# Feed-forward layers and a query projection: seven products over eight input tiles instead of four or six, with two of the weight sums made by adding transfers

## The chip, the core and the metric

The kernel runs on one core of one Trainium2 chip. The metric is device time in microseconds of the whole program, the median of several runs. On the core, TensorE (PE) multiplies, VectorE (DVE) and ScalarE (ACT) work element by element, GpSimd (POOL) does a few small operations, and the queues of SyncE (SP) and POOL issue transfers between memory and the chip.

## What is computed

The input is 256 rows of 2048 numbers in float32. Two layers follow each other. Cut to what matters here:

```python
D_MODEL = 2048; SEQ = 256; D_FF = 8192; N_HEADS = 16
def sq_relu_mlp(h, g, w1, w2):
    a = relu(rms_norm(h, g) @ w1)          # 2048 -> 8192
    return (a * a) @ w2                    # 8192 -> 2048
# layer 1: q, k, v, gate from one projection, causal attention with a forget bias
h = h + attention_1(h) @ a_w_out
h = h + sq_relu_mlp(h, mlp_norm_g[0], mlp_w1[0], mlp_w2[0])
# keys and values shared by what follows
k_sh, v_sh = split(rms_norm(h, kv_norm_g) @ kv_w)
# layer 2: own queries, chunked attention with a relative bias
q = rms_norm(rms_norm(h, b_norm_g) @ b_w_q)
h = h + attention_2(q, k_sh, v_sh) @ b_w_out
h = h + sq_relu_mlp(h, mlp_norm_g[1], mlp_w1[1], mlp_w2[1])
```

## The kernel before, in words

**Tiles.** The 256 rows are two blocks b of 128 (`NB`). The 2048 inputs of a product are 16 tiles of 128 (`KT`), its outputs panels of 512 columns. A weight comes in units of 128 x 1024 numbers (512 KB): two input tiles by one panel.

**Three passes.** Each unit is split into a coarse part `hi` (ScalarE, L210) and the rest `lo` (VectorE, L211) by `issue`, and activations are kept split in the same way. `passes` (L443 to L448) multiplies high by high, low by high and high by low; so a plain unit takes 2 blocks x 2 input tiles x 3 = 12 matmuls of 128 x 512. `fetch` (L220) keeps up to three split units ahead of TensorE (three `hi` and three `lo` buffers in pool `wsp`), and `EARLY` = 3 raw units loading beyond (`load`, L193, pool `wraw`, four buffers).

**Pairs in seven products.** In the feed-forward layers two neighbouring panels (1024 columns) make a `Pair` (L120). For the first n of the 16 input tiles the two row blocks by two panels are computed in seven products in place of eight, in Winograd's arrangement: blocks 11, 12, 21, 22 of the weight (input half by panel) and sums of them, T1 = 12 - 11, T3 = 22 - 12, T2 = T3 + 11, T4 = 21 - T2, each meet an activation block or a sum of activation blocks (`sums`, L262, kept in tiles `S` and `Sh`). The other 16 - n tiles are plain units, named a and b by panel. In the first weight n is 4 and a block is 1024 wide; in the second weight ("wide") n is 6 and a block is 1536 wide, split in one step of 1024 and one of 512 (`hih`, `loh`). `form_products` (L467) issues the matmuls of a block: 6 for 1024 numbers, 3 for 512.

`bring` (L777 to L779) loads whole blocks on the SP queue, `make` (L790) forms the sums T1 to T4 on VectorE, each pair at times given in `units` to each `Pair` (L153 to L165) and kept by `prepare`. Between the products the accumulators are folded: ScalarE copies them (L879, L882), VectorE adds (L861, L865).

**Chunks.** A feed-forward layer runs in four chunks (`NCH`) of 2048 hidden columns: two pairs of the first weight, then two pairs of the second, which use what the first two gave. `turn_hidden` (L825) transposes a finished panel in 32 x 32 pieces (L314), sends it out to memory and back (`turn`, L324 and L330), and `take` (L800) applies ReLU and square and splits (L803 to L814). The panels of the second weight are added to the rows h (L561). `plan_mlp` (L145) lists all units of a layer in order; the units b5 to b7 of a pair are put among the first products of the next.

**Other stages.** `panels` (L479) and `stage` (L496) run the other projections with plain units only, the query projection of layer 2 (`w_qb`, four panels) among them. Small work is handed out step by step through `fill` (`add_fill`, `run_fill`), one list of steps after each unit. `next_x` (L342) prepares the next stage's activations at the steps given in `LONG` and `SHORT`. `keep_order` (L36) holds DVE, ACT, PE and SP to the order in which the program is written, so an instruction that waits holds all that is behind it on its engine.

Of the kernel before, what the change touches and what calls it, by code (L numbers as in the profile page):

```python
# [15 lines left out]
P = 128  # L16
# [13 lines left out]
EARLY = 3  # L30
UA = UN // 512
REL = 384
WIDE = UN + 512
# [14 lines left out]
def trunk(ctx: ExitStack, tc: tile.TileContext, xT, xr, gs, hg, bf, wgate, w_in, w_oa, w1a, w2fa, w2sa,  # L48
          w_kv, w_qb, w_ob, w1b, w2fb, w2sb, rel, out):
# [9 lines left out]
    wraw = pool("wraw", 4)  # L59
    qkv = pool("qkv", 2)  # L60
    wk = pool("wk", 6)
# [46 lines left out]
    class Form:  # L108

        def __init__(self, pair, i, half):  # L110
            self.pair, self.name, self.half = pair, ("11", "T3", "T2", "T1", "21", "T4", "22")[i], half

    class Tail:

        fast = None

        def __init__(self, src, first):
            self.src = [[src[first + u] for u in range(KT // UA)]]

    class Pair:  # L120

        fast = True

        def __init__(self, big, src, order, third, units):
            self.big, self.src, self.third, self.units, self.order = big, src, third, units, order
            self.ps, self.t, self.wide, self.own = None, {}, order == "wide", 3 if order == "wide" else 2

        def items(self, names):
            return [(self, "abfh".index(i[0]), int(i[1])) for i in names.split()]

        def plan(self, rest):
            made = [self.items(f"f{i} h{i}" if self.wide else f"f{i}") for i in range(7)]
            own = {"early": "a2 F a3 F b2 F b3 a4 b4 a5 a6 a7", "": "a2 F a3 F a4 F a5 a6 a7 b2 b3 b4",
                   "wide": "a3 F b3 F a4 F b4 a5 a6 a7"}[self.order].split()
            plan = made[0] + rest[:1] + made[1] + rest[1:2] + made[2] + rest[2:] + made[3]
            n = 4
            for i in own:
                if i == "F":
                    plan += made[n]
                    n += 1  # L140
                else:
                    plan += self.items(i)
            return plan, self.items("b5 b6 b7")

    def plan_mlp(w1, w2f, w2s, tail):  # L145
        n, pairs = w1.shape[0] // NCH, []
        names = ("11", "12", "21", "22")
        for c in range(NCH):
            for q in range(2):
                at = c * n + 16 * q  # L150
                src = [[w1[at + 8 * j + u] for u in range(8)] for j in range(2)]
                order = "" if pairs else "early"
                when = (25, 20, 9, 15, 10, 8) if not pairs else (9, 7, 8, 6, 3, 2) if q and not c else (9, 7, 8, 6, 5, 1) if q else (7, 5, 6, 4, 3, 2)  # L153
                pairs.append(Pair({k: src[int(k[1]) - 1][int(k[0]) - 1] for k in names}, src, order, len(pairs) % 2 == 0, when))
            for q in range(2):
                at = 2 * c + q
                src = [[None] * 3 + [w2s[10 * at + 5 * j + u] for u in range(5)] for j in range(2)]
                when = (7, 5, 6, 4, 3) if q else (9, 7, 8, 6, 5) if c else (9, 7, 8, 6, 3)
                pairs.append(Pair({k: w2f[4 * at + i] for i, k in enumerate(names)}, src, "wide", len(pairs) % 2 == 0, when))
        plan, rest = [], [(tail, 0, u) for u in range(KT // UA - 3, KT // UA)]  # L160
        for p in pairs:
            mine, rest = p.plan(rest)
            plan += mine
        plan += rest
        units.extend(Form(p, i, q == 3) if q > 1 else p.src[q][i] for p, q, i in plan)  # L165
        return plan
# [3 lines left out]
    n_out = w_oa.shape[0] - 3  # L170
    queue(w_oa, n_out)
    tail_a = Tail(w_oa, n_out - 5)
    plan_a = plan_mlp(w1a, w2fa, w2sa, tail_a)
    queue(w_qb, w_qb.shape[0])
# [3 lines left out]
    tail_b = Tail(w_ob, n_out - 5)  # L178
    plan_b = plan_mlp(w1b, w2fb, w2sb, tail_b)
# [4 lines left out]
    def load(parts=1):  # L184
        src = units.popleft()
        if isinstance(src, Form):
            raws.append((src, ()))
            return
# [5 lines left out]
        raws.append((raw, cuts))  # L194

    def issue(parts=1):
        form = None
        if not raws:
            load(parts)
        raw, cuts = raws.popleft()  # L200
        if not cuts:
            form, half = raw, raw.half
            raw, cuts = form.pair.t[form.name], [slice(0, 512 if half else UN)]
            if half:
                raw = raw[:, UN:]
        n = cuts[-1].stop
        hi = wsp.tile([P, n], F32R, name="hi" if n == UN else "hih", bufs=3 if n == UN else 1)
        lo = wsp.tile([P, n], F32R, name="lo" if n == UN else "loh", bufs=3 if n == UN else 1)
        for c in cuts:
            S.activation(hi[:, c], raw[:, c], AF.Copy)  # L210
            V.tensor_tensor(lo[:, c], raw[:, c], hi[:, c].bitcast(F32), op=ALU.subtract)  # L211
        ready.append((hi, lo, n < UN))
        if form and form.name == "T3" and half == form.pair.wide:
            make(form.pair, "T2")

    def half_next():
        u = raws[0][0] if raws else units[0]
        return isinstance(u, Form) and u.half

    def fetch(ahead=AHEAD, early=EARLY):  # L220
        while (units or raws) and sum(1 for r in ready if not r[2]) <= ahead and not (half_next() and any(r[2] for r in ready)):
            issue()
        while units and sum(1 for r in raws if r[1]) < early:
            load()
        return ready.popleft()[:2]
# [14 lines left out]
    def acc_pair(which=None):  # L240
        if which is None:
            which, turns[0] = turns[0], 1 - turns[0]
        if which == 2:
            return [ps_s.tile([P, 512], F32, name="s") for _ in range(2)]
        return [ps_acc.tile([P, 512], F32, name="acc", tag=f"acc{which}{b}", bufs=1) for b in range(NB)]
# [16 lines left out]
    def sums(a, fs, n=2):  # L262

        w = [wk.tile([P, 512], F32, name="sum", tag="wk") for _ in range(n)]

        def part(i):
            at = i * n * P
            v = w[at // 512][:, at % 512 : at % 512 + n * P].rearrange("p (g t) -> p g t", g=n)
            return v.rearrange("p g (i c) -> p g i c", i=4) if len(a[0][0].shape) == 4 else v

        V.tensor_tensor(part(0), a[1][0], a[1][1], op=ALU.add)
        V.tensor_tensor(part(1), part(0), a[0][0], op=ALU.subtract)
        V.tensor_tensor(part(2), a[0][0], a[1][0], op=ALU.subtract)
        V.tensor_tensor(part(3), a[0][1], part(1), op=ALU.subtract)
        hi, lo = ([fs[k][:, i * 512 : (i + 1) * 512] for i in range(n)] for k in range(2))
        for i in range(n):
            S.activation(hi[i], w[i], AF.Copy)
        yield
        for i in range(n):
            V.tensor_tensor(lo[i], w[i], hi[i].bitcast(F32), op=ALU.subtract)  # L280
        yield

    def room(tag, name, dtype=F32):
# [729 lines left out]
```

## Time and profile before

| what | value |
|---|---|
| median of 3 runs | 2126.61 us (2125.93 to 2134.7) |
| profiled execution, from the first to the last instruction (its span) | 2124.3 us |
| PE, PEld, DVE busy | 2101.3, 1729.3, 1654.6 us |
| ACT, POOL busy | 1211.3, 49.1 us |
| granted TensorE clock, mean | 0.999 |
| moved by transfers | 491.63 MB, 231 GB/s on average |
| read from memory, written | 450.01 MB, 39.87 MB |

The first feed-forward layer runs from about 372 to 1062 us, the queries follow up to about 1115 us, keys, values and attention up to about 1390 us, and the second output projection and feed-forward layer fill the rest. A group's row gives line, engine, operation, output and inputs with their shapes, the count, then the busy time in us and the mean of one in ns, and last the idle time before them with what ended it. A timeline's row gives start, length, engine, line, operation and, in brackets, the idle time just before. PE's matmuls are pipelined: they overlap, and the time between their starts is what one costs.

### The profile page before, as it was taken

To read this page: it belongs to the slowest core of one execution; us is meant where nothing else is said; L and a number is where in the kernel's file an instruction comes from. 1 tells how busy PE (TensorE), PEld (TensorE's weight loads), DVE (VectorE), ACT (ScalarE), POOL (GpSimd) and SP (SyncE) were. 2 spreads that over 40 slices of the span, in tenths; PEclk is the share of its full clock that TensorE was granted. 3 is DMA by queue.
4 is the path that set the end of the run, shared out by engine and by line. 5 is a ranking of instruction groups with operands and counts; after the bars stand their busy time and mean duration, and the time that the engine had idled before them with its cause. 6 is when DMAs were issued, how large, how long until landed. Compare 5 with 4: busy or idle time off the path is not lost.

```text
span 2124.3 us, 26113 instructions
## 1 busy us (share of the span) xinstructions
PE 2101.3 (99%) x9278; PEld 1729.3 (81%) x9278; DVE 1654.6 (78%) x1931; ACT 1211.3 (57%) x1519; POOL 49.1 (2%) x48
## 2 busy tenths in 40 slices
PE   9999999999999999999999999999999999999999
PEld 7888888877888887888788888888788878878887
DVE  5767776888788878878877677678887887888786
ACT  6544445665566566556575454456654655665664
POOL 1001000000000000000001010000000000000000
PEclk9999999999999999999999999999999999999999
DMA  8787788776676576477577777787766766765763
GB/s 281 244 249 243 224 264 255 238 246 210 220 256 206 200 265 228 170 239 269 181 240 261 234 228 235 239 276 237 247 211 217 241 203 222 248 212 195 261 234 129
DMA packets 179283, 491.63 MB, mean 231 GB/s; under 512 B 36416, under 2 KB 73424, under 8 KB 179152
## 3 DMA queue, kind: packets, MB, share of 16 engines
q1 hardware_dynamic: 179152, 489.96, 69.8%
q8 instruction: 73, 1.20, 0.2%
q14 instruction: 58, 0.48, 0.1%
HBM read 450.01 MB, written 39.87 MB: 231 GB/s over the span
## 4 chain that ended last, share of the span: by engine, by line
PE 84%; DVE 7%; DMA 4%; ACT 2%; issue 2%; SPq 1%; ACTq 0%; DVEq 0%
PE acc L446 23%; PE acc L448 23%; PE acc L444 23%; PE s L444 4%; PE s L446 4%; PE s L448 4%; DVE lo L211 3%; ACT hi L210 2%; DVE w L790 1%; DVE loh L211 1%; DMA q<-turn 1%; DMA turn<-z 1%; DMA raw<-in_w_in 1%; DVE wT L790 1%; PE s L583 1%
## 5 line engine op out<-in xcount | busy, mean ns | idle before, releaser
L211 DVE TENSOR_TENSOR lo<-raw,hi 128x1024 fp32r<-128x1024 f32 (+1 forms) x610 | 738.2, 1215 | 260.1 <-ACT hi L210 253.0
L210 ACT ACTIVATE hi<-raw 128x1024 fp32r<-128x1024 f32 (+1 forms) x610 | 640.8, 1053 | 367.3 <-PE acc L446 266.8
L444 PE MATMUL acc<-hi,act 128*128 128x512 f32 x2208 | 608.4, 394 | 2.0 <-ACT hi L210 1.1
L446 PE MATMUL acc<-hi,act 128*128 128x512 f32 x2208 | 599.7, 390 | 6.4 <-DVE act L814 6.4
L448 PE MATMUL acc<-lo,act 128*128 128x512 f32 x2208 | 598.4, 390 | 0.0
L446 PEld LDWEIGHTS acc<-hi,act 128*128 128x128 f32 x2208 | 413.4, 188 | 98.2 <-DVE act L814 10.7
L448 PEld LDWEIGHTS acc<-lo,act 128*128 128x128 f32 x2208 | 413.3, 188 | 89.0 <-DVE lo L211 3.2
L444 PEld LDWEIGHTS acc<-hi,act 128*128 128x128 f32 x2208 | 412.9, 188 | 87.9 <-ACT hi L210 2.1
L210 ACT ACTIVATE hi<-w 128x1024 fp32r<-128x1024 f32 x160 | 169.1, 1057 | 226.4 <-DVE w L790 105.2
L211 DVE TENSOR_TENSOR lo<-w,hi 128x1024 fp32r<-128x1024 f32 x160 | 194.8, 1218 | 83.9 <-ACT hi L210 83.8
L444 PE MATMUL s<-hi,act 128*128 128x512 f32 x416 | 112.6, 389 | 0.0
L446 PE MATMUL s<-hi,act 128*128 128x512 f32 x416 | 112.5, 389 | 0.0
L448 PE MATMUL s<-lo,act 128*128 128x512 f32 x416 | 112.5, 389 | 0.0
L210 ACT ACTIVATE hi<-wT 128x1024 fp32r<-128x1024 f32 x64 | 67.7, 1057 | 54.9 <-DVE wT L790 27.9
L448 PEld LDWEIGHTS s<-lo,act 128*128 128x128 f32 x416 | 78.1, 188 | 16.2
L446 PEld LDWEIGHTS s<-hi,act 128*128 128x128 f32 x416 | 78.1, 188 | 16.2
L444 PEld LDWEIGHTS s<-hi,act 128*128 128x128 f32 x416 | 78.0, 188 | 16.2
L211 DVE TENSOR_TENSOR lo<-wT,hi 128x1024 fp32r<-128x1024 f32 x64 | 78.2, 1222 | 9.4 <-ACT hi L210 7.5
L210 ACT ACTIVATE hih<-w 128x512 fp32r<-128x512 f32 x80 | 49.8, 622 | 24.2 <-PE acc L446 16.0
L617 ACT ACTIVATE act<-po 128x256 fp32r<-128x256 f32 x32 | 12.3, 384 | 86.0 <-PE po L615 86.0
L211 DVE TENSOR_TENSOR loh<-w,hih 128x512 fp32r<-128x512 f32 x80 | 54.8, 685 | 7.3 <-ACT hih L210 7.3
L525 POOL TENSOR_TENSOR rn<-vv,mhalf 128x4 f32<-128x4 f32 x32 | 43.3, 1366 | 385.0 <-DVE vv L524 384.9
(190 smaller groups left out, 1717.0 us busy)
## 6 DMA issues: line engine op xcount, KB each, us to landing
raw<-in_w1a SPq DMA_DIRECT2D x96, 512.0 KB, 4.4
raw<-in_w1b SPq DMA_DIRECT2D x96, 512.0 KB, 4.5
raw<-in_w_in SPq DMA_DIRECT2D x94, 512.0 KB, 4.6
raw<-in_w2sa SPq DMA_DIRECT2D x80, 512.0 KB, 4.3
raw<-in_w2sb SPq DMA_DIRECT2D x80, 512.0 KB, 4.2
raw<-in_w_kv SPq DMA_DIRECT2D x64, 512.0 KB, 4.6
turn<-z SPq DMA_DIRECT2D x60, 512.0 KB, 4.2
w<-in_w2fa SPq DMA_DIRECT2D x32, 768.0 KB, 7.6
```

What stands on the lines that cost most here:

```text
L210: S.activation(hi[:, c], raw[:, c], AF.Copy)
L211: V.tensor_tensor(lo[:, c], raw[:, c], hi[:, c].bitcast(F32), op=ALU.subtract)
L444: TE.matmul(ps, xh, cut(hi, j), start=first, stop=False, **kw)
L446: TE.matmul(ps, xl, cut(hi, j), start=False, stop=False, **kw)
L448: TE.matmul(ps, xh, cut(lo, j), start=False, stop=last, **kw)
L525: G.tensor_tensor(rn, vv, mhalf, op=ALU.pow)
L583: TE.matmul(s[:, P : 3 * P], q[:, a, P:T], k[:, a], start=True, stop=True)
L617: S.activation(o[i][:, 0], po[:, :T], AF.Copy)
L790: V.tensor_tensor(d, a, b, op=op)
```

## The change

1. All pairs take n = 8: four tiles against four, blocks of 128 x 2048 ("11" to "22" in `f1a`, `f2a` and so on), each used in two halves s of 1024. A block half is one split step and 6 matmuls. The tile for `loh` and the 1536 wide blocks go. The activation sums are formed for both halves (`fs[0]`, `fs[1]`).
2. The query projection of layer 2 becomes two pairs as well, at the end of the first layer's plan.
3. The signs are arranged so that all sums of weights are additions: T3 = 12 + 22, T2 = T3 + 11, T1 = 11 + 12, T4 = T2 + 21. T3 and T1 are made by a transfer that adds block 22 (or 12) from memory into the tile of 12 (or 11), issued on the POOL queue. T2 and T4 stay on VectorE (L290, L260 of the new program). Blocks 21 and 22 as units of their own come through the raw buffers, so that 12 and 22 are read twice.
4. The order of the units is written out in `ORDER` for each kind of pair: f0 to f6 are the seven blocks (two halves each), a and b plain units, r the units left over from the pair before. What is brought, added and made after which unit, and how many units later, stands in `BEHIND`, and for the first pair of a layer in `OPENING`.
5. Accumulators alternate between `acc` and the banks of the pools `s` and `po`; two matmuls open two of them in the first pair of a layer. The last four units (before: three) of an output projection move into the plan behind it. Raw buffers: 6 for 4, `EARLY` 5 for 3, work buffers 5 for 6. The descriptor memory of POOL's queue is set to 8192.

In the program's order there are 8974 matmuls for 9138, 136 adding transfers on POOL, and 1269 transfers on SP for 1237; VectorE has 970 splits of 1024 for 830, none of 512 for 112, and 136 sums of weights of 1024 for 64 of 1024 and 64 of 1536.

```diff
-EARLY = 3
+EARLY = 5
+HIDDEN = ((1, 4, 7, 7, 8, 8, 10, 12), (1, 3, 7, 8, 8, 8, 11, 11), (1, 2, 5, 6, 6, 9), (0, 1, 4, 7, 7, 8))
+LONG = ((0, 0, 1, 3, 6, 7, 8, 8), (0, 0, 0, 1, 5, 5, 6, 6), (0, 0, 0, 0, 5, 6), (0, 0, 0, 2, 6, 6))
+SHORT = ((3, 0, 1, 3, 5, 5, 7, 8), (6, 1, 2, 5, 10, 10, 14, 14), (3, 0, 3, 4, 8, 10), (0, 0, 0, 2, 5, 5))
+ORDER = {
+    "first": "f0 r r f1 f2 r r f4 a4 f3 f5 b4 f6 a5 a6 r a7 b5",
+    "w10": "f0 r r f1 r f2 r f4 a4 a6 f3 a5 f5 f6 a7 b4 b5",
+    "w11": "f0 f1 r r f2 f4 a4 f3 a5 f5 f6 a6 a7 b4",
+    "w20": "r f0 r f1 f2 r f4 f3 f5 f6 a5 b4 a4 b5",
+    "w21": "f0 f1 f2 r f4 r f3 a5 r a4 b4 f6 r f5 a6",
...
+    "q0": "f0 r f1 r f2 f4 f3 r f6 f5 a4 b4 r b5 a5",
+    "q1": "f1 f0 r f2 r a4 f4 r r f3 a5 f6 f5",
+}
+BEHIND = {
+    (0, 0): [(0, 1, "make", 0)],
+    (0, 1): [(0, 1, "make", 1), (1, 1, "add", "T1", 1)],
+    (1, 0): [(3, 0, "bring", "12", 0)],
+    (1, 1): [(2, 0, "bring", "12", 1)],
+    (3, 0): [(2, 0, "bring", "11", 0)],
+    (3, 1): [(2, 0, "bring", "11", 1)],
+    (2, 0): [(1, 1, "add", "T1", 0)],
+    (6, 1): [(5, 0, "add", "T3", 1)],
+    (5, 0): [(2, 0, "add", "T3", 0)],
+}
...
-    wraw = pool("wraw", 4)
+    wraw = pool("wraw", 6)
-    wk = pool("wk", 6)
+    wk = pool("wk", 5)
...
     def issue(parts=1):
...
+        if item and item.u == 4:
+            assert (2, item.s) in item.pair.done
+            item.pair.done.add(("T4", item.s))
+            t = item.pair.t["T4"] = item.pair.t["T2"]
+            V.tensor_tensor(t[:, half(item.s)], t[:, half(item.s)], raw, op=ALU.add)
+        if item:
+            item.pair.done.add((item.u, item.s))
+            behind(item.pair, item.u, item.s)
+        if later:
+            for f in later.popleft():
+                f()
...
+    def bring(p, name, s):
+        assert not p.prev or p.prev.did(*((3,) if name == "11" else (1, "T2")))
+        p.done.add((name, s))
+        if not s:
+            p.t[name] = qkv.tile([P, BIG], F32, name="w" + name, tag="Y" if name == "11" else "X", bufs=1)
+        SY.dma_start(p.t[name][:, half(s)], p.big[name][:, half(s)])
+
+    def add(p, name, s):
+        to, block = {"T1": ("11", "12"), "T3": ("12", "22"), "T4": ("T2", "21")}[name]
+        p.t[name] = p.t[to]
+        assert (to, s) in p.done and (name == "T3" or {(0, s), ("T2", s)} <= p.done)
+        p.done.add((name, s))
+        G.dma_start(p.t[name][:, half(s)], p.big[block][:, half(s)], accum_op=ALU.add)
+
+    def make(p, s):
+        assert (not p.prev or p.prev.did(5)) and {("T3", s), ("11", s)} <= p.done
+        p.done.add(("T2", s))
+        if not s:
+            p.t["T2"] = qkv.tile([P, BIG], F32, name="wT2", tag="Z", bufs=1)
+        V.tensor_tensor(p.t["T2"][:, half(s)], p.t["T3"][:, half(s)], p.t["11"][:, half(s)], op=ALU.add)
+
+    later = deque()
+
+    def behind(p, i, s):
+        for d, own, f, *a in BEHIND.get((i, s), ()):
+            q = p if own else p.next
+            if q is not None:
+                while len(later) < d + 1:
+                    later.append([])
+                later[d].append(lambda f=f, q=q, a=a: {"make": make, "add": add, "bring": bring}[f](q, *a))
...
+    def form_products(p, hi, lo, i, s):
         items = []
+        for g in range(2):
             if i in (0, 4, 5):
+                xk = p.x[4 * s + g + 2 * (i > 0)]
+                xp = [xk[:, k, (i == 5) * P : (i == 5) * P + P] for k in range(2)]
             else:
+                c = (None, 2, 1, 0, None, None, 3)[i] * 2 * P + g * P
+                xp = [p.fs[s][k][:, c : c + P] for k in range(2)]
+            ps = p.ps[i in (1, 2, 3, 6)][i in (1, 5)]
+            items.append((ps, xp, g, i < 2 and s + g == 0, i < 2 and s + g == 2))
         passes(items, hi, lo, skip_group_check=True)
+        if s:
+            c = p.ps[1][0]
+            if i == 0:
+                S.activation(c, p.ps[0][0], AF.Copy, scale=-1.0)
+            elif i == 1:
+                p.P7 = wk.tile([P, 512], F32, name="p7", tag="wk")
+                S.activation(p.P7, p.ps[1][1], AF.Copy)
+            elif i == 2:
+                V.tensor_tensor(p.ps[0][1], p.P7, c, op=ALU.subtract)
+            elif i == 3:
+                V.tensor_tensor(p.ps[1][1], c, p.P7, op=ALU.subtract)
...
+            p.ps = [acc_pair(i) for i in ((2, 3), (0, 1))[count[0] % 2]]
...
+                if not p.prev:
+                    for ps in (p.ps[1][0], p.ps[0][1]):
+                        TE.matmul(ps, p.x[0][:, 0, :P], hl[0][:, :512], start=True, stop=True)
...
-    nc = bacc.Bacc("TRN2", target_bir_lowering=False, num_devices=1)
+    nc = bacc.Bacc("TRN2", target_bir_lowering=False, num_devices=1, dynamic_dma_scratch_size=8192)
```

In `BEHIND` a key is a block and its half; an entry gives how many units later, whether it is for the same pair (1) or the next (0), and what is done.

More of the change, by code (lines that the diff above doesn't have):

```diff
@@ L220, in fetch @@
+    later = deque()
[6 more added lines that the diff above has]
+                later[d].append(lambda f=f, q=q, a=a: {"make": make, "add": add, "bring": bring}[f](q, *a))
     def fetch(ahead=AHEAD, early=EARLY):
-        while (units or raws) and sum(1 for r in ready if not r[2]) <= ahead and not (half_next() and any(r[2] for r in ready)):
+        while (units or raws) and len(ready) <= ahead:
@@ L222, in fetch @@
             issue()
-        while units and sum(1 for r in raws if r[1]) < early:
+        while units and sum(1 for r in raws if r[2]) < early:
             load()
-        return ready.popleft()[:2]
+        return ready.popleft()
     fill = deque()
```

412 lines of the change are left out of this document (201 added, 211 removed), and 2 rows, old and new, of the table ORDER.

## The prediction

> **What bounds the kernel now.** I read the page's engine line first, then the chain, the costliest groups, and the table by stretches.
>
> ```profile
> PE 2101.3 (99%) x9278; PEld 1729.3 (81%) x9278; DVE 1654.6 (78%) x1931; ACT 1211.3 (57%) x1519; POOL 49.1 (2%) x48
> ...
> PE 84%; DVE 7%; DMA 4%; ACT 2%; issue 2%; SPq 1%; ACTq 0%; DVEq 0%
> ```
>
> TensorE is busy 99% of the span, and 84% of the chain that ended last is its matmuls. Busy matmuls overlap, so the price of one is read from where a run of them starts and ends:
>
> ```profile
> 707.24 1.07 PE L444 MATMUL acc<-hi,act 128*128 128x512 f32 x4
> 708.15 1.07 PE L446 MATMUL acc<-hi,act 128*128 128x512 f32 x4
> 709.06 1.07 PE L448 MATMUL acc<-lo,act 128*128 128x512 f32 x4
> 709.96 1.07 PE L444 MATMUL acc<-hi,act 128*128 128x512 f32 x4
> ```
>
> Twelve matmuls start within 2.72 us: **226.7 ns** each. A window of width w holds w/226.7 ns of them when nothing stalls; what is missing is stall. Columns: window, width, then busy time and count for PE, PEld, DVE, ACT, POOL, then clock, DMA share, GB/s.
>
> ```profile
> 371.80:1009.00 637.20, 630.31 (x2763) 516.84 (x2762) 527.58 (x537) 381.66 (x428) 0.00 (x0) 1.00 0.68 229
> 1009.00:1115.30 106.30, 104.43 (x461) 85.85 (x460) 81.28 (x86) 70.59 (x102) 2.71 (x3) 1.00 0.66 211
> 1390.00:2124.30 734.30, 723.07 (x3165) 593.26 (x3163) 597.07 (x609) 427.22 (x489) 0.00 (x0) 1.00 0.66 223
> ```
>
> Rows one and two are the first feed-forward layer and the end of it with the queries: 48 and 8 matmuls short of 2811 and 469, that is 10.9 and 1.8 us. Row three, the second layer, is 74 short (16.8 us), of which about 4 us is the store at the very end. So some **25 us** are stalls in the stages that the change touches. The rest of the kernel is not my subject.
>
> The stalls sit where the first product of a chunk turns into the second. From the chain in order of time (start, length, what):
>
> ```profile
> 455.25 4.81 DMA turn<-z
> 461.40 2.87 DMA q<-turn
> 466.46 1.77 DVE wT L790
> 480.33 4.21 DMA turn<-z
> 486.36 7.67 DMA q<-turn
> 502.52 1.20 PE acc L446 x4
> ```
>
> The hidden activations go out and back through memory while VectorE is also making weight sums (wT), and the matmul at 502.52 waits for them.
>
> **The change: matmuls.** One product of two row blocks by two column panels over n input tiles takes n/2 x 8 x 3 matmuls plainly and n/2 x 7 x 3 in seven products: 3n/2 fewer. Before, n is 4 in 16 pairs (first weight) and 6 in 16 pairs (second weight); after, n is 8 in all of these, and in 2 query pairs where it was 0. So 16 x 6 + 16 x 3 + 2 x 12 = 168 go; 4 come to open accumulators (2 in each layer); the program's order shows the same 164 (9138 to 8974). 164 x 226.7 ns = **37.2 us**. On the engine that bounds the span this comes off whole, as long as the others keep pace. The new matmuls have the old shape, so I give them the old price.
>
> **The change: VectorE.** Its rows, by form:
>
> ```profile
> L211 DVE TENSOR_TENSOR lo<-raw,hi 128x1024 fp32r<-128x1024 f32 x606 | 735.6, 1219 | 259.9 <-ACT hi L210 253.0 <-PE acc L446 3.2 <-DMA q<-turn 2.3
> L211 DVE TENSOR_TENSOR loh<-w,hih 128x512 fp32r<-128x512 f32 x80 | 54.8, 685 | 7.3 <-ACT hih L210 7.3
> L814 DVE TENSOR_TENSOR act<-q,act 128x1024 fp32r<-128x1024 f32 x32 | 39.0, 1218 | 0.0
> L314 DVE STREAM_TRANSPOSE z<-acc 128x512 f32<-128x512 f32 x48 | 31.4, 693 | 6.0 <-PE acc L448 6.0
> L790 DVE TENSOR_TENSOR w<-w,w 128x1536 f32<-128x1536 f32 x16 | 28.0, 1750 | 0.0
> L561 DVE SCALAR_TENSOR_TENSOR h<-acc,qm,h 128x512 f32<-128x512 f32 x24 | 16.9, 746 | 1.8 <-PE acc L448 1.7
> L790 DVE TENSOR_TENSOR w<-w,w 128x1024 f32<-128x1024 f32 x16 | 19.5, 1219 | 0.0
> L865 DVE TENSOR_TENSOR acc<-acc,p 128x512 f32<-128x512 f32 x16 | 11.1, 695 | 0.0
> L271 DVE TENSOR_TENSOR sum<-q 128x256 f32<-128x256 f32 x3 | 1.3, 418 | 0.0
> L271 DVE TENSOR_TENSOR sum<-q 128x128 f32<-128x128 f32 x3 | 0.9, 287 | 0.0
> ```
>
> I count one chunk: two pairs of the first weight and two of the second.
> - Before: 72 splits of 1024 (87.8), 14 of 512 (9.6), 8 sums of 1024 and 8 of 1536 (23.8), 8 folds of accumulators (5.5), 8 transposes (5.6), 4 squares' low parts (4.9), 8 residuals (6.0), activation sums (4 x 0.418 + 4 x 0.287 + 3 x 0.69 = 4.9): 148.1 us.
> - After: 4 x 22 = 88 splits (107.3), 16 sums of 1024 (two of the four blocks' sums have gone to transfers; 19.5), folds, transposes, low parts and residuals as before (22.0), activation sums (8 x 0.418 + 4 x 0.69 = 6.1): 154.9 us.
>
> TensorE's part of the chunk falls from 738 matmuls (167.3 us) to 720 (163.2 us). Rows of VectorE that follow each other closely overlap:
>
> ```profile
> 796.58 1.18 DVE L211 TENSOR_TENSOR lo<-raw,hi 128x1024 fp32r<-128x1024 f32 x1
> 797.68 1.22 DVE L814 TENSOR_TENSOR act<-q,act 128x1024 fp32r<-128x1024 f32 x1
> 798.81 1.22 DVE L211 TENSOR_TENSOR lo<-w,hi 128x1024 fp32r<-128x1024 f32 x1
> 799.95 0.29 DVE L271 TENSOR_TENSOR sum<-q 128x128 f32<-128x128 f32 x1
> ```
>
> ```profile
> 1858.80:1911.90 53.10, 52.08 (x229) 42.41 (x228) 46.09 (x45) 32.33 (x40) 0.00 (x0) 1.00 0.64 212
> ```
>
> Three of 1.2 us start 1.10 to 1.14 us apart. In the first layer VectorE is busy 527.6 of 637.2 us, 82.8%; of a chunk's real 170.4 us (167.3 and a share of the stalls) that is 141.1, or 0.953 of the sum of rows. After, 0.953 x 154.9 = 147.6 of 163.2 us: **90%**. No 40th of the span now shows more than 46.09 of 53.1 us (87%, last row above), and that slice is 5 matmuls short (1.1 us). VectorE gets close to being the bound; the mixing of units of two pairs, one needing 6 and one 12 matmuls for the same split, is what keeps its load even, and with the old order I would expect the sums to stall TensorE.
>
> So the 25 us of stalls are not simply gone. The turn from first to second product gets units of the next pair to hide behind, and that removes most of them; the denser VectorE puts others in. With no stall at all the span would be 2124.3 - 37.2 - 25 = 2062 us. I take about 1 us for each of the 28 slices of 53.1 us in these stages, as the slice at 1858.80 has: 28 us. Ends: 0, and VectorE never above 87%: 147.6/0.868 = 170.0 us a chunk, 6.8 above 163.2, 8 chunks, 54 us.
>
> **The change: transfers.** Block 12 and block 22 are read twice, 2 MB more for each of 34 pairs, and 136 of the transfers of 512 KB add into a tile. No row of before adds, so its price is bounded by the plain ones. The middle of the first layer, and a stretch with the queue full:
>
> ```profile
> q1 hardware_dynamic: 33319, 108.67, 66.2%
> raw<-in_w1a SPq DMA_DIRECT2D x72, 512.0 KB, 4.3
> raw<-in_w2sa SPq DMA_DIRECT2D x55, 512.0 KB, 4.4
> w<-in_w2fa SPq DMA_DIRECT2D x24, 768.0 KB, 7.4
> w<-in_w1a SPq DMA_DIRECT2D x22, 512.0 KB, 4.6
> ```
>
> ```profile
> 788.00:796.00 8.00, 8.00 (x37) 6.64 (x36) 7.47 (x9) 5.99 (x7) 0.00 (x0) 1.00 1.01 402
> ```
>
> Full, the engines move 402 GB/s: 1.30 us for 512 KB. The weights of that window (478 us) are 97.0 MB, 241 of 316 busy us; the other 75 us belong to 12 panels of activations, 6.3 each. A pair after has 16 plain transfers (20.8 us), on average one panel (6.3) and four adding ones, against 40.8 us of matmuls. If an add costs what a copy costs, the engines are 79% busy; at twice (it reads its target too), 92%. I take twice and no loss: the T3 add of the next pair has some 24 us from the release of its tile to its use, T1 the 13.6 us of eight units, against 4.4 us to landing. If one were late, VectorE's sum T2 would wait for T3 (or ScalarE's split for T1), all later splits of the unit order would queue behind it, and TensorE would run out after at most three units. From 2.6 times on (3.4 us) transfers set the pace.
>
> Where I cost an edit at nothing: 32 more issues on SP, at 0.4 us and early; six raw buffers for four (5 loads ahead) cover a load that waits behind a block's tile; one work buffer fewer, touched by short-lived tiles only (0 to 2 us). On POOL nothing but adds is queued in these stages. The query pairs' norms and stores keep their work.
>
> **Sum.** 2062 + 28 = 2090 us of span; the median lies 2.3 us above the span (2126.6 to 2124.3): **2092 us**.
>
> **Rivals.**
> - *VectorE sets the pace*: 2062 + 54 = 2116, with the median at 2118; at 85% busy it would be 173.6 us a chunk and 2147. Against it: rows without a gap, as at 796. Chance 0.22, spread from 2104 to 2150.
> - *The stalls vanish*, even load and early activations: 2064 to 2078. Chance 0.12.
> - *Slower: the adding transfer is dear.* The place is the sixteen transfer engines, the price 34 x (27.1 + 4A - 40.8) us above 2062. It passes the time before from A = 3.9 us, three times a copy; at four times (5.2) it gives 2062 + 241 = 2303. For it: no adding transfer is in the trace. [...] Chance 0.13.
> - [...] Chance 0.08, from 2105 to 2150. [...]
>
> **How the numbers follow.** Forecast, 2078 to 2104: 0.45. With the rivals (0.22, 0.12, 0.13, 0.08) that is 1. A measurement tells about 0.5% from no change: 2116 and 2137. Faster: 0.45 + 0.12 + 0.12 + 0.02 = 0.71; same: 0.06 + 0.03 = 0.09; slower: 0.13 + 0.04 + 0.03 = 0.20. The range 2066 to 2137 leaves out the slower cases and the lowest few.
>
> **What would show it.** 8974 matmuls at 226.7 ns; VectorE near 48 of 53.1 us in feed-forward slices; DMA share 0.9 or more there, an adding transfer's landing under 10 us; the turns of the hidden activations gone from the chain. Wrong if the sums of VectorE wait for POOL's queue, if DMA share stands at 1.0 with TensorE waiting, or if 53.1 us slices hold fewer than 228 matmuls.

## The result, and the profile after

The changed kernel takes **2139.68 us**, median of 5 runs (2137.72 to 2142.62), against 2126.61 us (2125.56 to 2134.7, 5 runs). The ratio is 1.006, with a 95% interval of 1.0043 to 1.0077: slower by 0.6%. The forecast was 2092 us, faster. The profiled execution has a span of 2140.9 us and a mean granted clock of 0.994 (before: 2124.3 us and 0.999).

The page of the kernel after: the engine line, the transfer engines' share in 40 slices, and the two queues that carry the data (packets, MB, share of 16 engines).

```profile
PE 2087.9 (98%) x9114; PEld 1701.5 (79%) x9114; DVE 1733.5 (81%) x2003; ACT 1311.4 (61%) x1567; POOL 167.6 (8%) x184
...
DMA  8787779999899899899987877798998998998995
...
q1 hardware_dynamic: 183760, 489.96, 68.8%
q0 software_dynamic: 19584, 71.31, 18.7%
```

PE has 9114 matmuls for 9278, so the 164 are gone. Queue q0 is new: it is POOL's, with the 136 adding transfers. They hold 18.7% of sixteen engines' span, 0.187 x 2140.9 / 136 = **2.94 us of all engines for each** 512 KB, where a plain copy took 1.30 us.

The table by stretches of the kernel after (columns as in the prediction): first the two feed-forward stages whole, the first one with the queries, then four slices of a fortieth of the span.

```profile
374.00:1124.00 750.00, 722.79 (x3101) 582.15 (x3100) 646.29 (x655) 492.26 (x536) 59.52 (x69) 0.99 0.92 271
...
1392.00:2080.00 688.00, 668.87 (x2888) 541.94 (x2888) 582.46 (x590) 443.31 (x477) 52.02 (x61) 0.99 0.93 273
```

```profile
535.23:588.75 53.52, 53.52 (x237) 44.18 (x236) 43.45 (x41) 31.54 (x31) 3.45 (x4) 1.00 0.81 252
588.75:642.27 53.52, 51.51 (x217) 40.92 (x216) 45.21 (x47) 33.76 (x35) 4.30 (x5) 0.97 0.97 274
642.27:695.79 53.52, 51.50 (x223) 41.05 (x222) 48.30 (x49) 38.65 (x42) 6.06 (x7) 1.00 0.94 267
...
1070.45:1123.97 53.52, 49.19 (x206) 38.88 (x205) 46.85 (x53) 37.47 (x50) 3.44 (x4) 0.97 0.89 250
```

A full slice holds 236 matmuls. One slice is full; the others are 13 to 30 short, that is 3 to 7 us of 53.5, and in two of them the granted clock is 0.97.

To compare kernels I sum what lies between the starts of PE's matmuls beyond 226.7 ns each, over the rows of PE's timeline in the feed-forward and query stages. I call this sum the **gaps**. It contains waits and also matmuls at a lower clock.

| kernel | span, us | gaps, us | span less gaps |
|---|---|---|---|
| before | 2124.3 | 26.3 | 2098.0 |
| after | 2140.9 | 80.1 | 2060.8 |

The last column fell by 37.2 us. So the matmuls that were taken out are worth what was forecast, and the loss is in the gaps: 54 us more. (Such a sum is good to one or two us, so the agreement to the tenth is luck.) Of the 80.1 us, 26 gaps of over 1 us make 41.9; the rest are small ones and slow matmuls. The clock's part is an estimate: 0.994 for 0.999 is 0.005 x 2140.9 = 11 us. The profiled execution is the slowest of the five and has the lowest clock; the other four stand at 0.996 to 0.998, where the same estimate gives 2 to 6 us.

**Where the gaps are.** They recur at the same places in most of the eight chunks. A chunk in the middle of a layer takes about 170 us, as it did before, although it has 18 matmuls (4.1 us) fewer. The largest gap, in six chunks, is in the first pair of a chunk. PE's timeline there:

```profile
623.36 0.61 PE L542 MATMUL acc<-lo,act 128*128 128x512 f32 x2
625.81 0.73 PE L538 MATMUL acc<-hi,S 128*128 128x512 f32 x2 [1.83 <-ACT hi L253]
626.38 0.84 PE L540 MATMUL acc<-hi,S 128*128 128x512 f32 x2
627.07 1.22 PE L542 MATMUL acc<-lo,S 128*128 128x512 f32 x2
628.09 1.06 PE L538 MATMUL acc<-hi,S 128*128 128x512 f32 x2
```

It waits for a split of ScalarE. ScalarE's timeline, with one row of VectorE's in between, says why that one is late:

```profile
613.19 1.06 ACT L896 ACTIVATE q<-q 128x1024 f32<-128x1024 f32 x1 [1.79 <-DMA q<-turn]
...
616.32 1.23 DVE L254 TENSOR_TENSOR lo<-w,hi 128x1024 fp32r<-128x1024 f32 x1 [1.37 <-ACT hi L253]
...
618.09 2.00 ACT L253 ACTIVATE hi<-wT 128x1024 fp32r<-128x1024 f32 x2
623.51 1.30 ACT L361 ACTIVATE Sh<-sum 128x512 fp32r<-128x512 f32 x2 [3.43 <-DVE sum L356]
624.72 3.88 ACT L253 ACTIVATE hi<-raw 128x1024 fp32r<-128x1024 f32 x4
```

ScalarE waits 1.79 us for the turned hidden activations. The split behind that wait is late and VectorE idles 1.37 us for it. From then on VectorE works without a gap, reaches the activation sums only at 622.60, and ScalarE waits 3.43 us more at their copy (L361). Four splits stand behind that copy in ScalarE's order, though nothing of theirs depends on it.

The second place, in seven chunks, is in the first pair of the second weight, where PE waits for VectorE itself:

```profile
658.48 0.62 PE L540 MATMUL po<-hi,Sh 128*128 128x512 f32 x2
660.36 0.73 PE L542 MATMUL po<-lo,Sh 128*128 128x512 f32 x2 [1.26 <-DVE lo L254]
```

```profile
653.88 1.22 DVE L260 TENSOR_TENSOR wT<-wT,raw 128x1024 f32<-128x1024 f32 x1
655.02 0.69 DVE L583 TENSOR_TENSOR s<-p,po 128x512 f32<-128x512 f32 x1
655.62 1.22 DVE L254 TENSOR_TENSOR lo<-raw,hi 128x1024 fp32r<-128x1024 f32 x1
656.75 1.22 DVE L260 TENSOR_TENSOR wT<-wT,raw 128x1024 f32<-128x1024 f32 x1
657.89 1.31 DVE L397 STREAM_TRANSPOSE z<-acc 128x512 f32<-128x512 f32 x2
659.12 2.32 DVE L254 TENSOR_TENSOR lo<-w,hi 128x1024 fp32r<-128x1024 f32 x2
```

VectorE has no gap in these rows: from 653.88 to 659.12 us it makes two T4 sums, a fold and two transposes, and one single split. Half a block gives TensorE 6 matmuls, 1.36 us, for a split that takes VectorE 1.14; with a sum beside the split VectorE needs 2.28, so it falls behind at that place unless units split in advance or a plain unit cover the difference, whatever its mean load is.

Waits over the whole kernel after (total us, times, longest), and the median us to landing of some transfers:

```profile
ACT q L896 <- DMA q<-turn: 50.5, 22, 5.7
ACT Sh L361 <- DVE sum L356: 37.6, 16, 3.4
```

```profile
raw<-in_s1a SPq DMA_DIRECT2D x64, 512.0 KB, 7.1
...
q<-turn SPq DMA_DIRECT2D x168, 128.0 KB, 6.6
...
w<-in_f1a POOLq DMA_DIRECT2D x32, 512.0 KB, 8.3
```

The same waits of the kernel before:

```profile
ACT Sh L277 <- DVE sum L274: 28.3, 8, 4.7
ACT Sh L277 <- DVE sum L272: 16.7, 8, 2.1
ACT q L803 <- DMA q<-turn: 15.6, 8, 3.4
```

ScalarE waited for the activation sums then too, 45.0 us in all, and in these stages none of TensorE's gaps of over 0.4 us ended with a split of ScalarE. New is that the wait for the turned activations has tripled and comes just ahead. In the kernel before, `raw` of the feed-forward weights landed after 4.2 to 4.5 us and `q<-turn` after 4.7. The adding transfers land in 8.3 to 8.8 us in the feed-forward layers, and neither VectorE's sums nor ScalarE's splits are seen to wait for one; but the plain ones beside them have become slow.

### The profile page after: what moved, and what is told of

It is laid out like the page before. It is cut to its first block, busy times and chain, and to the rows that moved or that the text cites. A ratio compares the mean times of both kernels' runs of the same rounds, so it can differ in the third digit from the quotient of the medians.

```text
span 2140.9 us, 26525 instructions
## 1 busy us (share of the span) xinstructions
PE 2087.9 (98%) x9114; PEld 1701.5 (79%) x9114; DVE 1733.5 (81%) x2003; ACT 1311.4 (61%) x1567; POOL 167.6 (8%) x184
## 3 DMA queue, kind: packets, MB, share of 16 engines
q0 software_dynamic: 19584, 71.31, 18.7%
## 5 line engine op out<-in xcount | busy, mean ns | idle before, releaser
L538 PE MATMUL acc<-hi,act 128*128 128x512 f32 x1644 | 462.4, 397 | 4.7 <-ACT hi L253 2.8
L540 PE MATMUL acc<-hi,act 128*128 128x512 f32 x1644 | 450.0, 390 | 0.0
L542 PE MATMUL acc<-lo,act 128*128 128x512 f32 x1644 | 448.8, 390 | 0.0
L538 PEld LDWEIGHTS acc<-hi,act 128*128 128x128 f32 x1644 | 306.7, 189 | 71.8 <-DVE acc L583 4.8
L540 PEld LDWEIGHTS acc<-hi,act 128*128 128x128 f32 x1644 | 309.0, 188 | 66.1 <-DVE act L343 1.0
L542 PEld LDWEIGHTS acc<-lo,act 128*128 128x128 f32 x1644 | 308.4, 188 | 65.1 <-DVE lo L254 0.6
L254 DVE TENSOR_TENSOR lo<-w,hi 128x1024 fp32r<-128x1024 f32 x204 | 245.1, 1215 | 24.8 <-ACT hi L253 24.7
L254 DVE TENSOR_TENSOR lo<-wT,hi 128x1024 fp32r<-128x1024 f32 x136 | 163.4, 1221 | 22.8 <-ACT hi L253 20.9
L253 ACT ACTIVATE hi<-wT 128x1024 fp32r<-128x1024 f32 x136 | 140.9, 1053 | 30.5 <-PE po L540 14.6
L260 DVE TENSOR_TENSOR wT<-wT,raw 128x1024 f32<-128x1024 f32 x68 | 82.8, 1218 | 0.0
L290 DVE TENSOR_TENSOR wT<-w,w 128x1024 f32<-128x1024 f32 x68 | 82.8, 1218 | 0.0
L538 PE MATMUL po<-hi,act 128*128 128x512 f32 x272 | 73.0, 390 | 0.4 <-ACT hi L253 0.4
L540 PE MATMUL po<-hi,act 128*128 128x512 f32 x272 | 72.7, 389 | 0.0
```

What stands on the lines that cost most here:

```text
L260: V.tensor_tensor(t[:, half(item.s)], t[:, half(item.s)], raw, op=ALU.add)
L290: V.tensor_tensor(p.t["T2"][:, half(s)], p.t["T3"][:, half(s)], p.t["11"][:, half(s)], op=ALU.add)
L538: TE.matmul(ps, xh, cut(hi, j), start=first, stop=False, **kw)
L540: TE.matmul(ps, xl, cut(hi, j), start=False, stop=False, **kw)
L542: TE.matmul(ps, xh, cut(lo, j), start=False, stop=last, **kw)
```

## The experiments

Two theories stood at the start. **A**: the adding transfers fill the engines, so all that is loaded comes late. **B**: VectorE, with more to do in a shorter chunk, is late. A third, **C**, came from the rows above: the place of single instructions in ScalarE's order turns a small lateness into a stop. All kernels are edits of the kernel after unless another is named. Ratios are to the kernel before, measured beside each; differences in us are between medians taken at different times, in which the kernel before itself lay between 2124.9 and 2127.5 us.

**1. Without the adding transfers** (the blocks 12 and 22 are not added; T1 and T3 stay 11 and 12).

```diff
-        G.dma_start(p.t[name][:, half(s)], p.big[block][:, half(s)], accum_op=ALU.add)
```

> The changed kernel without its 136 adding transfers: block 12 stands in for T3 and block 11 for T1, so the weight sums are left out of the result; everything else is as in the changed kernel. Theory A (the transfers are what was missed: two blocks read twice, each adding transfer 2.9 us of all engines, everything lands late): the share of the transfer engines in the feed-forward slices falls from 0.95 to about 0.75, raw units land in 4.5 instead of 7.1 us, and the time falls to about 2095 us. Theory B (VectorE and ScalarE, busy to 90% and in a fixed order, hold each other up): the time stays within 12 us of the changed kernel's 2140.

Measured: 2109.11 us, 0.992 (0.9903 to 0.9936). Its page and its landings:

```profile
PE 2074.6 (98%) x9114; PEld 1697.5 (81%) x9114; DVE 1735.2 (82%) x2003; ACT 1313.4 (62%) x1567; POOL 50.7 (2%) x48
```

```profile
raw<-in_s1a SPq DMA_DIRECT2D x64, 512.0 KB, 5.0
```

```profile
ACT q L895 <- DMA q<-turn: 13.2, 10, 5.0
```

VectorE's load is the same, these loads land in 5.0 us, and the kernel is 30.6 us faster. The transfers cost that much; but 47.0 us of gaps are left, so they are not all of it.

**2. The adds as plain copies** (same bytes read, same queue; the copy replaces the tile instead of adding to it).

```diff
-        G.dma_start(p.t[name][:, half(s)], p.big[block][:, half(s)], accum_op=ALU.add)
+        G.dma_start(p.t[name][:, half(s)], p.big[block][:, half(s)])
```

> The changed kernel with its 136 adding transfers made plain copies of the same blocks on the same POOL queue: block 22 overwrites 12, and 12 overwrites 11, so the sums are left out of the result. Same bytes read, no reading of the target. Theory A: a copy takes some 1.4 us of the engines against 2.9, the share falls to about 0.85 and the time to about 2115 us. Theory B: within 8 us of 2140.

Measured: 2110.24 us, 0.993 (0.9913 to 0.9948).

```profile
q0 software_dynamic: 19584, 71.31, 10.7%
```

```profile
374.00:1110.00 736.00, 719.41 (x3128) 583.59 (x3127) 652.21 (x660) 496.88 (x540) 37.67 (x70) 1.00 0.84 278
```

```profile
ACT q L896 <- DMA q<-turn: 25.8, 10, 4.5
```

A copy on POOL's queue takes 0.107 x 2109.8 / 136 = 1.66 us of all engines, an add 2.94. Reading the blocks a second time costs 1 us, which is within the noise; that the transfer adds costs 29. So a busy share of 0.84 was nearly free and one of 0.92 was not. The turned activations land no earlier than with the adds (`q<-turn` 6.7 us with copies, 6.6 with adds, 6.0 without either), but ScalarE's wait for them is half as long. That wait is not the measure of the loss either: in experiment 3 it is 51.0 us, as in the kernel after, and the time is 34.7 us less.

**3. Without VectorE's weight sums** (T2 and T4 formed in 64 of 1024 columns only; the tile of T2 is set up and filled once per layer in place of once per pair, which the lines below leave out).

```diff
-            V.tensor_tensor(t[:, half(item.s)], t[:, half(item.s)], raw, op=ALU.add)
+            c = slice(item.s * UN, item.s * UN + 64)
+            V.tensor_tensor(t[:, c], t[:, c], raw[:, :64], op=ALU.add)
...
-        V.tensor_tensor(p.t["T2"][:, half(s)], p.t["T3"][:, half(s)], p.t["11"][:, half(s)], op=ALU.add)
+        c = slice(s * UN, s * UN + 64)
+        V.tensor_tensor(p.t["T2"][:, c], p.t["T3"][:, c], p.t["11"][:, c], op=ALU.add)
```

> The changed kernel with its sums T2 and T4 on VectorE cut to the first 64 of 1024 columns (the rest of the sum is left out of the result): 136 instructions of 1.22 us become short, 16 to 17 us less VectorE work for each chunk of 163 us; all transfers stay, the adding ones too. Theory A: within 10 us of 2140. Theory B: VectorE falls from 90 to 80 per cent, most stalls of the feed-forward stages go, and the time falls to about 2095 us.

Measured: 2105.02 us, 0.99 (0.9886 to 0.9915), 34.7 us faster than the kernel after.

```profile
PE 2070.2 (99%) x9114; PEld 1696.5 (81%) x9114; DVE 1607.9 (77%) x2003; ACT 1310.3 (62%) x1567; POOL 170.4 (8%) x186
...
q0 software_dynamic: 19584, 71.31, 18.7%
```

The adding transfers are all there at the same price, and the gaps at `po<-lo,Sh` are gone.

**4. Neither** (the edits of 1 and 3).

> Both at once: no adding transfers, and T2 and T4 cut to 64 columns (these sums are left out of the result). Both theories: near the time without stalls, 2062 to 2085 us. If it stays above 2110, neither theory holds and the loss is in the order of the units or in the waits for the activations. If the two cuts add up, the causes are independent; if either alone gives most of it, it is slack that is missing.

Measured: 2083.71 us, 0.9803 (0.9788 to 0.9817); gaps 20.2 us, clock 1.000. Alone the two gave 30.6 and 34.7, together 56.0 us: nearly the sum. So A and B are each about half of the loss, and neither replaces the other. Part of each gain is the clock, which stands at 0.998 to 1.000 in the profiles of experiments 1 to 4: the kernel after has seven stretches at half the clock (see the last section), these four have two, none, one and none. So this part counts in the gain of either half and only once in the two together, which fits that 56.0 is less than 65.3.

**5. The copies of the activation sums one unit later.**

```diff
-    def sums(a, fs):
+    def sums(a, fs, late=False):
...
         V.tensor_tensor(part(3), a[0][1], part(1), op=ALU.subtract)
+        if late:
+            yield
...
-HIDDEN = ((1, 4, 7, 7, 8, 8, 10, 12), (1, 3, 7, 8, 8, 8, 11, 11), (1, 2, 5, 6, 6, 9), (0, 1, 4, 7, 7, 8))
+HIDDEN = ((1, 4, 7, 7, 8, 8, 10, 11, 12), (1, 3, 7, 8, 8, 8, 10, 11, 11), (1, 2, 5, 6, 6, 9), (0, 1, 4, 7, 7, 8))
```

> The changed kernel with one thing moved: ScalarE's two copies of the hidden activations' sums (they wait for VectorE to form the sums, and every later split waits behind them) are put one unit later than the sums, so that VectorE is done when ScalarE comes to them. Nothing is left out. Theory C (the stall of 1.0 to 2.0 us once a chunk ahead of the block products of the first weight is this wait, and TensorE runs slow for some us behind each long one): these eight sites go, 10 to 20 us less than the changed kernel, 2120 to 2130 us. Theory D (that stall is only where the lack of VectorE time comes out): it moves elsewhere, and the time stays within 5 us of 2140.

Measured: 2129.45 us (10 runs), 1.0012 (0.9999 to 1.0024); gaps 63.6 us, clock 0.998. The gaps at `acc<-hi,S` are gone and a shorter one, 1.3 us at `acc<-lo,act`, is in most chunks instead. Theory C holds for about 10 us, some of which can be the clock (0.998 for 0.994 to 0.998).

**6. The hidden activations taken up one unit later as well** (on 5; a later first step of `take` in all four panels).

```diff
-HIDDEN = ((1, 4, 7, 7, 8, 8, 10, 11, 12), (1, 3, 7, 8, 8, 8, 10, 11, 11), (1, 2, 5, 6, 6, 9), (0, 1, 4, 7, 7, 8))
+HIDDEN = ((1, 4, 8, 8, 9, 9, 10, 11, 12), (1, 3, 8, 8, 9, 9, 10, 11, 11), (1, 2, 6, 7, 7, 9), (0, 1, 5, 7, 7, 8))
```

> As the run before, and ScalarE's first step on a finished panel of hidden activations (it waits for their way out to memory and back, 50 us in all in the changed kernel, 26 with plain copies) is put one unit later for every panel. Nothing is left out. If the loss from the adding transfers comes through this wait, ScalarE's wait for the returning panels falls under 25 us and the time by another 5 to 12 us; if not, the wait falls and the time stays within 4 us of the run before.

Measured: 2131.27 us, 1.0019 (1.0003 to 1.0035). No gain. Its waits:

```profile
ACT hi L253 <- DMA raw<-in_s2b: 23.8, 4, 7.0
ACT hi L253 <- DMA raw<-in_s2a: 21.7, 4, 5.8
```

The wait for `q<-turn` has left the top of the list, and waits for plain weight units stand there. ScalarE was not asking too early: whatever it asks for next is late.

**7. Units not interleaved** (all units left over from the pair before come first, then the products, then the plain units).

```diff
-    "w10": "f0 r r f1 r f2 r f4 a4 a6 f3 a5 f5 f6 a7 b4 b5",
-    "w11": "f0 f1 r r f2 f4 a4 f3 a5 f5 f6 a6 a7 b4",
+    "w10": "r r r r f0 f1 f2 f4 f3 f5 f6 a4 a6 a5 a7 b4 b5",
+    "w11": "r r f0 f1 f2 f4 f3 f5 f6 a4 a5 a6 a7 b4",
...
```

> The changed kernel with the interleaving undone: in each pair but the first of a layer, the units left over from the pair before come first, then the seven blocks with nothing between them, then the plain units. Same instructions, same transfers, nothing left out. If the interleaving is what keeps VectorE (1.1 us a block half and the sums against 1.36 us of matmuls) in step, 14 block halves in a row need about 22 us of VectorE for 19 of TensorE, and each of the 34 pairs loses 1 to 3 us more: 2170 to 2240 us. If it does nothing, within 8 us of 2140.

Measured: 2208.83 us, 1.0377 (1.0358 to 1.0397); gaps 130.3 us. The order with interleaving is worth 69 us in this kernel; some 16 of them lie outside the stages in which the gaps are summed (the span less gaps is 2076.7 us).

**8. T1's products ahead of those of block 21 in the first wide pair** (on 5), to move the T4 sums away from the fold.

```diff
-    "w20": "r f0 r f1 f2 r f4 f3 f5 f6 a5 b4 a4 b5",
+    "w20": "r f0 r f1 f2 r f3 f4 f5 f6 a5 b4 a4 b5",
```

> As the late copies, and in the first pair of the second weight the block T1 goes ahead of T4, so that VectorE's sum T4 and the transposes of the finished hidden panel no longer fall into the same two units, where TensorE waits 1.4 us for a split in every chunk. Nothing is left out. If VectorE's crowding at that spot is the cause, the seven sites of 1.4 us go, 6 to 15 us less than the late copies alone; if VectorE simply lacks the time in this pair, the wait moves a few units on and the time stays within 4 us.

Measured: 2144.72 us, 1.0072 (1.005 to 1.0094), 15 us worse than 5. Neither forecast was right. The gap of 1.4 us went elsewhere (`s<-lo,act` up to 1.4 us, `po<-hi,act` up to 1.8) and there are more of them. That agrees with VectorE being short of time at that place whatever the order, but other orders were not tried.

**9 and 10. The T4 sum, then both sums, on POOL** (on 5).

```diff
-            V.tensor_tensor(t[:, half(item.s)], t[:, half(item.s)], raw, op=ALU.add)
+            G.tensor_tensor(t[:, half(item.s)], t[:, half(item.s)], raw, op=ALU.add)
```

> The kernel of e5 with the T4 sum (the one in the w20 stage's preparation) on POOL in place of VectorE; nothing is left out of the computation. Leaving both vector sums out gave 34.7 us (e3), so half of that, 10 to 17 us, is the most that this one can give. Theory D (POOL's sum runs beside VectorE and costs only POOL's own time): 2112 to 2120, the wait 'po<-lo,Sh' gone. Theory E (POOL and VectorE get in each other's way, or POOL's sum is slow enough, above about 2.5 us per 1024 columns, to make the T4 tiles late): 2129 or more, with longer VectorE instructions or TensorE waiting for POOL.

> The kernel of e5 with both vector sums (T2 and T4) on POOL; nothing is left out of the computation. Theory D: 2095 to 2106, near e3's 2105 with e5's 10 us on top at best, faster than before by 1%. Theory E: 2135 or more, worse than e9, because POOL also issues the adding transfers and those queue behind its sums.

Measured: 2176.85 us, 1.0232 (1.0211 to 1.0254), and 2227.48 us, 1.0463 (1.0439 to 1.0487), that is 47 and 98 us more than 5. Theory E, they get in each other's way. The groups of the kernel with T4 on POOL, from POOL and from VectorE:

```profile
L260 POOL TENSOR_TENSOR wT<-wT,raw 128x1024 f32<-128x1024 f32 x68 | 217.5, 3240 | 145.3 <-issue 136.6 <-DVE lo L254 8.6
```

```profile
L254 DVE TENSOR_TENSOR lo<-raw,hi 128x1024 fp32r<-128x1024 f32 x630 | 882.9, 1420 | 218.4 <-ACT hi L253 203.6 <-PE s L544 5.0 <-PE po L542 4.1
```

POOL takes 3.24 us where VectorE took 1.22, and VectorE's splits grow from 1218 to 1420 ns: it lost 83 us of sums and got 127 us of longer splits. Two timelines of the same stretch show how:

```profile
652.75 6.60 POOL L260 TENSOR_TENSOR wT<-wT,raw 128x1024 f32<-128x1024 f32 x2 [5.95 <-issue]
```

```profile
651.38 2.36 DVE L254 TENSOR_TENSOR lo<-wT,hi 128x1024 fp32r<-128x1024 f32 x2
653.98 6.46 DVE L254 TENSOR_TENSOR lo<-raw,hi 128x1024 fp32r<-128x1024 f32 x2 [0.24 <-ACT hi L253]
```

Two splits that took 2.36 us just before, most of that time ahead of POOL's pair, take 6.46 us beside the pair of 6.60. That the adding transfers queue behind POOL's sums, the other reason that was forecast for the second kernel, is not shown by these rows.

**11. Without the query pairs** (on 5; the query projection in plain units in a stage of its own, 24 matmuls more).

```diff
-    plan_a = plan_mlp((f1a, s1a), (f2a, s2a), (fqb, sqb), tail_a)
+    plan_a = plan_mlp((f1a, s1a), (f2a, s2a), None, tail_a)
+    queue(w_qb, w_qb.shape[0])
...
+    stage(xb, [query(g) for g in range(NG)], (2, 3))
```

> The kernel of e5 with the second query panel pairs undone: the query projection goes back to plain panels in a stage of its own, 24 matmuls more, which is 24 x 226.7 ns = 5.4 us. In the kernel after, the gaps between 1065 and 1117 us sum to about 9 us. If those gaps are the pairs' own price, the plain query gives 2124 to 2128; if they come from the end of the layer whichever way the query is computed, 2133 to 2137.

Measured: 2124.93 us (10 runs), 0.9985 (0.9971 to 1.0), 4.5 us faster than 5 although it has 5.4 us more of matmuls. The five gaps of 1.3 to 1.8 us at the query pairs (8.2 us) are gone. So that part of the change costs more than it saves, by an amount that is only just clear of the noise of the two ratios.

**12. A seventh raw buffer** (on 11).

```diff
-EARLY = 5
+EARLY = 6
...
-    wraw = pool("wraw", 6)
+    wraw = pool("wraw", 7)
-    wk = pool("wk", 5)
+    wk = pool("wk", 4)
-    sm = pool("sm", 6)
+    sm = pool("sm", 3)
```

> The kernel of e11 with a seventh raw buffer and six units loading ahead in place of five (paid for with one work buffer and three sets of small norm tiles). If single late landings stop TensorE (the engines are 0.92 busy but a unit more in advance would bridge a burst), one unit more, 2.7 us of cover, takes away most of the 5 to 10 us that e11 still loses to transfers: 2114 to 2120. If the loss sits in the order of VectorE's and ScalarE's work or in the turned activations, which a raw buffer does not help, 2123 to 2128.

Measured: **2118.37 us** (9 runs), 0.9968 (0.9953 to 0.9983); gaps 46.8 us, clock 1.000. Its page:

```profile
q0 software_dynamic: 18432, 67.12, 17.9%
```

One unit more in advance gives 6.6 us by the medians and 3.6 by the ratios, whose intervals overlap. The adding transfers are still at 2.9 us each (0.179 x 2114.6 / 128 = 2.96), and `raw<-in_s1a` still lands in 7.2 us. The time lies where it was forecast if a part of A is bursts that a deeper store of units bridges, but the gain is too near to the noise to show that. This kernel is 0.3% faster than the one before. More units in advance were not tried.

## Why the prediction was wrong

- **The matmuls** (37.2 us, price 226.7 ns each): right. 164 are gone, and the span less gaps fell by 37.2 us. The floor without a stall, 2062 us, is what four of the experiments show too: span less gaps is 2061.2 without the adds, 2063.2 without the sums, 2060.7 without both, and 2063.7 with the later copies.
- **The stalls after, "about 1 us for each of the 28 slices", 28 us**: this is the step that failed. They are 80 us (77 at the median time). The size was taken from one slice of a kernel whose transfer engines stood at 0.64 to 0.68 and whose VectorE had slack. The two ends of the term were 0 and 54 us, so even its upper end was too low, because it had a price for VectorE alone and none for the transfers, the queries and the clock. That a chunk does take the 170 us of that upper end is luck: without the adding transfers (experiment 1) it takes 167.
- **The adding transfer, "twice and no loss"**: the price was close. An add takes 2.94 us, 2.3 times the 1.30 us that was read from a stretch with a full queue and 1.8 times the 1.66 us of a copy on its own queue, and the busy share is 0.92 to 0.93 where 92% was forecast. Twice was my estimate; what makes an add dearer than a copy is not shown by the runs. "No loss" was wrong by 29 us (experiments 1 and 2). I compared the landing of an add with the time until its use, and it does land in under 10 us. What is late is the rest in the same engines: plain units land in 7.1 us, in 5.8 with copies in place of the adds and in 5.0 without them. Which of these late loads carries the loss is not shown: taking the wait for the turned activations away gave nothing (experiment 6).
- **VectorE at 90%**: right as an amount of work and the wrong measure. A chunk holds 146 us of VectorE's work (from 625.8 to 796.3 us) where 147.6 were forecast; its share is 86%, because the chunk became longer than the 163.2 us forecast. Among the blocks TensorE needs a new split every 1.36 us, and VectorE with a sum in between cannot give it. The sums cost 35 us (experiment 3).
- **The turn hidden behind units of the next pair**: the interleaving helps (69 us, experiment 7), and still the wait of ScalarE for `q<-turn` rose from 15.6 to 50.5 us. The adding transfers account for most of the rise (25.8 us with copies, 13.2 without them), though the landing by itself, 6.6 us, is the same with copies.
- **ScalarE's order** was in no step. The copy at L361 holds four splits that don't need it; 10 us (experiment 5).
- **The query pairs** were counted with their 24 matmuls and nothing else; they cost about 10 us (4.5 and the 5.4 of the matmuls, experiment 11), of which 8.2 are gaps of over 1 us.
- **The rivals.** *VectorE sets the pace* and *the adding transfer is dear* each named a half; I took them as alternatives, and they add up: 30.6 and 34.7 us alone, 56.0 together. The second had the right engines and the wrong point: the loss does not begin where transfers set the pace (3.4 us an add in the prediction's sum, and 3.9 to be as slow as before), but already at 2.94. The chance of 0.08 was for VectorE held up while POOL issues an add; no run shows such a loss. POOL spends 0.85 to 0.87 us on issuing each of the 136, and VectorE's splits keep their length:

```profile
L254 DVE TENSOR_TENSOR lo<-raw,hi 128x1024 fp32r<-128x1024 f32 x630 | 756.2, 1218 | 236.2 <-ACT hi L253 222.3 <-PE s L540 4.1 <-DMA pbuf<-turn 1.5
```

  This is 1218 ns on the kernel after, 1219 before.

What stays open: how the 47 us of gaps in the best version are shared between the last of the late transfers and VectorE's crowding. In it the gaps at `po<-lo,Sh` (1.4 us) and `acc<-lo,act` (1.3 us) are still in nearly every chunk, and the first of them was removed by taking VectorE's sums away. Its gaps of over 0.4 us make 33 us, and 30 of these end with a split of VectorE; how far ScalarE's wait for the turned activations (60.6 us there) makes those splits late is not known.

## What to carry to other kernels

Work that is taken off the bound engine is only worth its full price if the engines that feed it keep their slack at each place: compare the feeder's time per unit with the consumer's time per unit in the densest stretch, not over a chunk. A transfer's price is not only whether it lands in time itself, but also how much later it makes its neighbours: here a busy share of 0.92 in place of 0.84 made plain loads of 512 KB land in 7.0 to 7.3 us in place of 5.8 to 7.0, and the kernel 29 us slower. Two rivals that need different resources should be priced as a sum too, since both can be true.

## What the runs showed of the hardware

- **An adding transfer** of 512 KB takes 2.94 us of all sixteen engines, a copy from the same queue 1.66 (experiment 2). POOL spends 0.85 to 0.87 us on issuing one.
- **The clock fell after some short gaps.** The table by stretches of 2 us behind the gap at 624 us of the kernel after (clock, DMA share and GB/s are the last three columns):

```profile
624.00:626.00 2.00, 0.19 (x1) 0.19 (x2) 0.36 (x2) 1.96 (x4) 0.00 (x0) 1.00 1.02 251
626.00:628.00 2.00, 2.00 (x6) 1.32 (x6) 2.00 (x2) 2.00 (x3) 0.00 (x0) 0.65 1.11 183
628.00:630.00 2.00, 2.00 (x6) 1.52 (x5) 2.00 (x3) 0.60 (x1) 0.00 (x0) 0.50 1.04 218
630.00:632.00 2.00, 2.00 (x11) 1.61 (x10) 2.00 (x4) 1.60 (x2) 0.00 (x0) 0.99 1.03 367
```

  TensorE stood still for 1.83 us and then, from 626.6 us on, ran at half its clock for about 3.4 us (the clock column adds up to that): the pairs of matmuls that start at 627.07 and 628.09 are 1.02 us apart, in place of 0.45. Not each such gap does this. The same view behind the gap of 1.8 us at 475 us:

```profile
475.00:477.00 2.00, 0.40 (x3) 0.07 (x1) 1.72 (x4) 1.97 (x4) 0.00 (x0) 1.00 1.01 219
477.00:479.00 2.00, 1.94 (x8) 1.28 (x9) 2.00 (x2) 1.82 (x3) 0.00 (x0) 1.00 1.11 210
```

  There the clock stays at 1.00. The trace of the kernel after has seven such slow stretches, behind idle times of 1.5 to 2.4 us, and that of the kernel before one, though it has a gap of 2.13 us without any; so the length of the gap alone does not decide it, and what else does is not shown. Seven stretches at half the clock cost 7 x 1.7 = 12 us, an estimate that agrees with the 11 us above.
- **VectorE's splits took longer beside POOL's sums.** Beside POOL's pair of 6.60 us two splits of VectorE took 6.46 us, for 2.36 us just before (experiment 9), and the mean of 630 splits there is 1420 ns, for 1218 in the kernel after. The adding transfers, which POOL only issues in 0.85 to 0.87 us each, showed nothing of the kind: the splits take 1218 ns with them.
